# Pinning the up projection's products in program order on TensorE, and shifting on-chip memory from kept activations to raw weight buffers

## The chip, the cores and the metric

One core of a Trainium2 chip runs the whole kernel. The metric is the device time of one execution in microseconds (us). Three executions of the kernel before took 2089.94, 2092.08 and 2092.11 us; their median, 2092.08, is the time before. The engines are TensorE (PE, with its weight loads PEld), VectorE (DVE), ScalarE (ACT), GpSimd (POOL) and SyncE (SP); POOL and SP only issue DMAs where this change is concerned.

## The reference

One layer of an encoder: 512 tokens of 2048 features, in float32. The change touches only the gated MLP in the second half.

```python
xn = rms_norm(x, ffn_norm_g)                   # x: 512 x 2048
up = xn @ w_up                                 # w_up: 2048 x 11264
up = depthwise_conv(up, ffn_dw_w, ffn_dw_b)    # width 3, along the tokens
gate, val = split(up, 2)                       # 5632 channels each
x = x + (silu(gate) * val) @ w_down            # w_down: 5632 x 2048
return rms_norm(x, final_norm_g)
```

Ahead of it stand an input projection, a depthwise convolution and a neighbourhood attention, and an output projection.

## The kernel before

**Precision.** The products must come out in float32. A weight tile (`raw`, 128 x 1024, 512 KB) arrives by DMA. ACT rounds it into `whi` (L115), and DVE takes the remainder into `wlo` (L116), each 128 x 1024. Activations are split likewise. A product is then made of two or three matmuls: high by high, high by low, low by high. There are `NW` = 4 buffers for `whi` and for `wlo`, and `NR` = 7 for `raw`.

**The up projection.** A loop over 44 passes `f` (`hidden`, called in the loop near L747) makes 128 gate channels and 128 value channels for all 512 tokens in each. It doesn't multiply the blocks of weights and activations directly but uses seven products of sums of blocks, as in Strassen's scheme, in the order `TURN` = (3, 2, 4, 5, 1, 0, 6). The activation sums `xc` are made once and kept in SBUF. The weight sums are made by accumulating DMAs on POOL (L601) and additions on DVE (L611, L613). Each product but 2 takes eight steps `k` of two matmuls: L652 (`whi`, 512 columns) and L653 (`wlo`, 256 columns). Product 2 runs through the helper `mm3` (L126, L127, L128): eight steps of three matmuls of 256 columns.

**PSUM in a pass.** `ea` is one tile of two banks, whose halves are `pe` and `pa` (L637 to L639); `pd_`, `pb` and `pc_` are tiles of one bank. Products 3, 4 and 1 add up in `pa`, product 2 in `pc_`, 5 in `pd_`, 0 in `pe`, 6 in `pb`. After 3, 4 and 1, ACT copies what `pa` holds so far to `pd_`, `pe` and `pb` (`copied`, L660). After product 5 the two halves of `pd_` are added to the gate `g`; after product 0 `ea`, both its banks, to the value `vl`; and after product 6 `pb` to the rest of `g`. These folds are an ACT copy (L663) and a DVE addition (L664). ACT copies product 2's result to `w` (L670). So product 3 of the next pass writes `pa` only when the fold of `ea` has read it.

**What sets the order.** The kernel is written in program order, and a scheduler gives each engine its own order by priorities: it may move an instruction ahead of others if its operands are there. `shifted(-100)` raises the priority of the copies at L660. `pin` (`keep_in_program_order`) holds an instruction in its place among the pinned ones of its engine. Weights are asked for by `weights()`: whenever a product begins, the `whi` and `wlo` of the product `AHEAD` = 3 places later are made, and accumulating DMAs are begun `FAR` = 8 places ahead. `tick` and `done` put other work behind a product's last matmul: the steps that make the MLP's normalising factor in the first pass (statistics at L212, factors L215 to L225, L228), and the sums of the down projection's weights on POOL (L177, L180).

**The first pass.** The output projection ends just ahead of it, and the last of the `xc` that product 3 and the others multiply are still being made then (L542 on ACT, L543 on DVE).

**The MLP's activations.** A pass ends with the norm's factor, the convolution of width 3 and silu times value, which give one 2 KB tile per partition of `h` (128 x 512). The first 36 are stored to DRAM by SP (L708). The last `KEEP` = 8 stay in SBUF. In the last pass, POOL reloads the 36 (L741), up to eight behind each product. They come from a pool of `NT` = 79 tiles of 2 KB.

**The down projection** goes over 22 pairs of `h` in each of seven products (`TURN2`), kept pairs first (`order2`), with matmuls at L768 to L770. Its operand `ho` is made by `operand` (L730, L731) from `h` or from sums of halves of `h` (`hc`).

Of the kernel before, what the change touches and what calls it, by code (L numbers as in the profile page):

```python
# [39 lines left out]
KC0 = [0, 8, 24, 32]  # L40
H = S // 2
NK = NF // 2
KEEP = 8
NT = 79
NR = 7
AHEAD = 3
FAR = 8
NW = 4
# [22 lines left out]
def layer(ctx: ExitStack, tc: tile.TileContext, xT, w_in, w_out, w_up, w_down, par, tab, g3, out):  # L71
    nc = tc.nc
    consts = ctx.enter_context(tc.tile_pool(name="consts", bufs=1))
    wpool = ctx.enter_context(tc.tile_pool(name="w", bufs=3))
    tp = ctx.enter_context(tc.tile_pool(name="t", bufs=NT))
    sm = ctx.enter_context(tc.tile_pool(name="sm", bufs=2))
# [4 lines left out]
    @contextmanager  # L81
    def shifted(by):

        at = tc.cur_priority
        tc.cur_priority = max(at + by, 0)
        yield
        tc.cur_priority = at + (tc.cur_priority - max(at + by, 0))

    def t2(name, dt=F32):
        return tp.tile([P, S], dt, tag="t2k", name=name)  # L90

    def t4(shape, name):

        return wpool.tile(shape, F32, tag="raw", name=name, bufs=NR)

# [12 lines left out]
    def raw_unit(src, n):  # L108
        raw = t4([P, U * P], "raw")
        return raw, nc.sync.dma_start(raw[:, :n], src)  # L110

    def parts(raw, n):
        hi = wpool.tile([P, U * P], F32R, tag="whi", name="whi", bufs=NW)
        lo = wpool.tile([P, U * P], F32R, tag="wlo", name="wlo", bufs=NW)
        i = nc.scalar.activation(hi[:, :n], raw[:, :n], AF.Copy)  # L115
        j = nc.vector.tensor_sub(lo[:, :n], raw[:, :n], hi[:, :n].bitcast(F32))  # L116
        return hi, lo, i, j

    def unit(src, n):

        return parts(raw_unit(src, n)[0], n)[:2]

    def mm3(ps, w, wk, mh, ml, start, stop, more=False):
        hi, lo = w[:2]
        a = slice(wk * P, (wk + 1) * P)
        nc.tensor.matmul(ps, hi[:, a], mh, start=start, stop=False, skip_group_check=more)  # L126
        nc.tensor.matmul(ps, hi[:, a], ml, start=False, stop=False, skip_group_check=more)  # L127
        return nc.tensor.matmul(ps, lo[:, a], mh, start=False, stop=stop, skip_group_check=more)  # L128

# [3 lines left out]
    def tick(behind):  # L133
        for todo in (steps, asteps):
            while todo:
                try:
                    with tc.issue_after(behind.ins):
                        next(todo[0])
                    break
                except StopIteration:  # L140
                    todo.pop(0)
# [5 lines left out]
    def weights():  # L147
        at = weights.at
        weights.at += 1
        for i in range(at, min(at + 1 + FAR, len(plan))):  # L150
            if i in sums:
                sums.pop(i)()
        while len(made) < min(at + 1 + AHEAD, len(plan)):
            made.append(plan[len(made)]())
        return made[at]
# [90 lines left out]
    pin = tc.keep_in_program_order  # L246
    first = [w_in[n, :, u * U * P:(u + 1) * U * P] for u in range(KD // U) for n in (NC_, 0)]
    for k in range(KD):
# [6 lines left out]
        if k in (0, 2, 6, 15):  # L255
            raw, i = raw_unit(first[len(early)], U * P)
            pin(i)
            w = parts(raw, U * P)
# [6 lines left out]
    for step in ORDER:  # L265
        i = next(a_ if step == "a" else q_)
# [326 lines left out]
    def factors(f, at):  # L593

        def load(q):
            a["q", q] = raw_unit(w_up[f, q], U * P)[0]
            return a["q", q]

        def summed(c, q1, q2):
            a[c] = raw_unit(w_up[f, q1], U * P)[0]  # L600
            nc.gpsimd.dma_start(a[c], w_up[f, q2], accum_op=ALU.add)  # L601

        def make(c):
            if c in plain and ("q", plain[c]) not in a:
                load(plain[c])
            if c in plain:
                return a["q", plain[c]]
            if c == 1:
                return a[1]
            if c == 4:  # L610
                add(a[2], a[2], load(A22))  # L611
            elif c == 6:
                add(a[2], a[2], a["q", A12])  # L613
            return a[2]

        a = {}
        plain = {0: A22, 3: A11, 5: A12}
        sums[at + TURN.index(2)] = lambda: summed(2, A21, A11)
        sums[at + TURN.index(1)] = lambda: summed(1, A22, A21)
        return [lambda c=c: parts(make(c), U * P)[:2] for c in TURN]  # L620

    add = nc.vector.tensor_add
    for f in range(NF):
        plan.extend(factors(f, len(plan)))
    order2 = [*range(NK - KEEP // 2, NK), *range(NK - KEEP // 2)]
    def unit2(c, k):
        return unit(wsum[c][k] if c in wsum else w_down[k, {0: A22, 3: A11, 5: A12}[c]], U * P)
# [15 lines left out]
    def up(f, done):  # L643

        def product(c, ps, more):
            hi, lo = wt = weights()
            for k in range(U):
                m, w = comb[c][k], slice(k * P, (k + 1) * P)
                if c == 2:
                    i = mm3(ps[:, :H], wt, k, m[:, :H], m[:, H:], k == 0, k == U - 1)  # L650
                    continue
                nc.tensor.matmul(ps, hi[:, w], m, start=k == 0 and not more, stop=False, skip_group_check=more)  # L652
                i = nc.tensor.matmul(ps[:, :H], lo[:, w], m[:, :H], start=False, stop=k == U - 1,  # L653
                                     skip_group_check=more)
            tick(i)
            done(TURN.index(c), i)

        def copied(to, ps):
            with shifted(-100):
                nc.scalar.activation(to, ps, AF.Copy)  # L660

        def folded(to, ps):
            nc.scalar.activation(to, ps[..., H:], AF.Copy)  # L663
            add(to, to, ps[..., :H])  # L664

        product(3, pa, False)
        copied(pd_, pa)
        product(2, pc_, False)
        w = t2("w")[:, :H]
        nc.scalar.activation(w, pc_[:, :H], AF.Copy)  # L670
        product(4, pa, True)
        copied(pe, pa)
        product(5, pd_, True)
        g = t2("g")
        folded(g[:, :H], pd_)
        product(1, pa, True)
        copied(pb, pa)
        product(0, pe, True)
        v = t2("vl")
        by = v.rearrange("p (i t) -> p i t", i=2)  # L680
        folded(by, ea)
        add(by, by, w.unsqueeze(1).broadcast_to([P, 2, H]))
        product(6, pb, True)
        folded(g[:, H:], pb)
        return g, v
# [11 lines left out]
    hs = [None] * NF  # L697
    hd = [dram.tile([P, S], F32, name=f"h{f}") for f in range(NF - KEEP)]

    def hidden(f, done):  # L700
        g, v = up(f, done)
        nc.vector.tensor_mul(g, g, rstd2[0])
        nc.vector.tensor_mul(v, v, rstd2[0])
        g, v = conv3(g, f), conv3(v, NF + f)
        nc.scalar.activation(g, g, AF.Silu)
        nc.vector.tensor_mul(g, g, v)
        if f < NF - KEEP:
            nc.sync.dma_start(hd[f], g)  # L708
        else:
            hs[f] = g  # L710

    def operand(c, k):

        (b11, b12), (b21, b22) = ((hs[i][:, :H], hs[i][:, H:]) for i in (2 * k, 2 * k + 1))
        if c in (3, 5, 6):
            src = {3: b11, 5: b21, 6: b22}[c]
        else:
            t = t2("hc")
            src, m = t[:, :H], t[:, H:]
            if c == 2:  # L720
                nc.vector.tensor_sub(src, b22, b12)
            elif c == 1:
                nc.vector.tensor_sub(src, b11, b12)
            else:
                nc.vector.tensor_sub(m, b11, b12)
                nc.vector.scalar_tensor_tensor(src, b22, -1.0, m, op0=ALU.mult, op1=ALU.subtract)
                if c == 0:
                    nc.vector.scalar_tensor_tensor(src, src, -1.0, b21, op0=ALU.mult, op1=ALU.subtract)
        t = t2("ho", F32R)
        nc.scalar.activation(t[:, :H], src, AF.Copy)  # L730
        nc.vector.tensor_sub(t[:, H:], src, t[:, :H].bitcast(F32))  # L731
        return t

    back = [f for p in range(2) for f in range(p, NF - KEEP, 2)]

# [11 lines left out]
    for f in range(NF):  # L747
        hidden(f, again if f == NF - 1 else paced)
    assert not jobs and not open_job and not back

    def four(first):

        if first:
            b = psa.tile([P, 2, S], F32, tag="sc", name="pd2")
            return [b[:, 0], b[:, 1]] + [psa.tile([P, S], F32, tag="tr", name="pd", bufs=2) for _ in range(2)]
        return [psm.tile([P, S], F32, tag="mm", name="pd") for _ in range(3)] + [psa.tile([P, S], F32, tag="po",
                                                                                         name="pd")]
# [97 lines left out]
    a = four(True)  # L857
# [19 lines left out]
    a = four(True)  # L877
# [68 lines left out]
```

## Time and profile before

| | |
|---|---|
| median of three runs | 2092.08 us |
| the profiled execution, its span | 2091.84 us, 2090.1 us |
| mean granted clock of TensorE, as a share of full speed | 0.996 |
| DMA, mean over the span | 213 GB/s, 444.72 MB |
| up projection, about | 708 to 1656 us of the span |
| down projection, about | 1657 to 2082 us of the span |

How to read the rows: a row of the page's groups has the line, the engine, the operation, output and inputs with shapes and count, then busy time and mean ns of one, then the idle time of the engine just ahead of these instructions and what ended it (`<-`). A row of waits has the engine and line that waited, what ended the wait, the total in us, how many times and the longest. A row of the timeline has the start and the duration in us, the engine and line, and in brackets the idle time ahead and its releaser. Matmuls are pipelined: their rows overlap, and one that starts 0.12 us after another may be given 0.28 us.

### The profile page before, as it was taken

To read this page: it belongs to the slowest core of one execution; us is meant where nothing else is said; L and a number is where in the kernel's file an instruction comes from. 1 tells how busy PE (TensorE), PEld (TensorE's weight loads), DVE (VectorE), ACT (ScalarE), POOL (GpSimd) and SP (SyncE) were. 2 spreads that over 40 slices of the span, in tenths; PEclk is the share of its full clock that TensorE was granted. 3 is DMA by queue.
4 is the path that set the end of the run, shared out by engine and by line. 5 is a ranking of instruction groups with operands and counts; after the bars stand their busy time and mean duration, and the time that the engine had idled before them with its cause. 6 is when DMAs were issued, how large, how long until landed. Compare 5 with 4: busy or idle time off the path is not lost.

```text
span 2090.1 us, 28359 instructions
## 1 busy us (share of the span) xinstructions
PE 2015.7 (96%) x10511; PEld 1687.4 (81%) x10511; DVE 1602.6 (77%) x2267; ACT 1090.8 (52%) x1680; POOL 228.5 (11%) x314
## 2 busy tenths in 40 slices
PE   8999999999999999999999999999999999999997
PEld 6888888877788788888888888888888788888886
DVE  7985796686558787777878777787878798895765
ACT  6234424447426665555555555565655554554553
POOL 0111111110011111111111111111110300000000
PEclk9999999999999999999999999999999999999999
DMA  6777677767658788888888888888886776665563
GB/s 228 171 222 181 179 172 193 182 181 239 187 165 216 195 217 249 216 237 236 225 253 208 253 216 245 228 237 241 214 239 160 283 275 219 211 213 194 193 207 132
DMA packets 140859, 444.72 MB, mean 213 GB/s; under 512 B 15792, under 2 KB 23984, under 8 KB 139312
## 3 DMA queue, kind: packets, MB, share of 16 engines
q1 hardware_dynamic: 97776, 292.94, 40.4%
q0 software_dynamic: 42944, 149.97, 34.0%
q8 instruction: 82, 1.34, 0.2%
q14 instruction: 57, 0.47, 0.1%
HBM read 425.02 MB, written 110.10 MB: 256 GB/s over the span
## 4 chain that ended last, share of the span: by engine, by line
PE 74%; issue 20%; ACT 3%; DMA 1%; DVE 1%; POOL 0%; SPq 0%; POOLq 0%; DVEq 0%; ACTq 0%
PE pu L652 24%; PE pu L653 12%; PE pj L126 6%; PE pj L128 6%; PE pj L127 6%; PE po L126 3%; PE po L127 3%; PE po L128 3%; ACT whi L115 3%; PE pu L126 3%; PE pu L128 2%; PE pu L127 2%; PE po L450 1%; PE sc L410 1%; PE trp L437 1%
## 5 line engine op out<-in xcount | busy, mean ns | idle before, releaser
L115 ACT ACTIVATE whi<-raw 128x1024 fp32r<-128x1024 f32 x574 | 606.9, 1058 | 867.7 <-PE pu L652 310.7
L116 DVE TENSOR_TENSOR wlo<-raw,whi 128x1024 fp32r<-128x1024 f32 x574 | 697.2, 1221 | 377.3 <-ACT whi L115 354.5
L652 PE MATMUL pu<-xc,whi 128*128 128x512 f32 x2112 | 760.5, 403 | 1.5 <-ACT pu L660 1.5
L653 PE MATMUL pu<-xc,wlo 128*128 128x256 f32 x2112 | 593.1, 281 | 0.0
L652 PEld LDWEIGHTS pu<-xc,whi 128*128 128x128 f32 x2112 | 396.7, 188 | 103.8 <-ACT pu L660 9.9
L653 PEld LDWEIGHTS pu<-xc,wlo 128*128 128x128 f32 x2112 | 399.0, 189 | 0.3 <-issue 0.2
L126 PE MATMUL pj<-xh,whi 128*128 128x512 f32 x640 | 253.9, 398 | 8.7 <-ACT whi L115 8.7
L128 PE MATMUL pj<-xh,wlo 128*128 128x512 f32 x640 | 251.0, 392 | 0.6 <-DVE wlo L116 0.5
L127 PE MATMUL pj<-xl,whi 128*128 128x512 f32 x640 | 251.2, 393 | 0.0
L768 PE MATMUL pd<-whi,ho 128*128 128x512 f32 x616 | 240.2, 390 | 1.6 <-ACT ho L730 1.6
L770 PE MATMUL pd<-whi,ho 128*128 128x512 f32 x616 | 240.2, 390 | 0.6 <-DVE ho L731 0.6
L769 PE MATMUL pd<-wlo,ho 128*128 128x512 f32 x616 | 240.3, 390 | 0.0
L324 DVE SCALAR_TENSOR_TENSOR y<-ch,prm,y 128x507 f32<-128x507 f32 (+14 forms) x240 | 169.9, 741 | 3.3
L126 PEld LDWEIGHTS pj<-xh,whi 128*128 128x128 f32 x640 | 120.8, 189 | 37.1 <-ACT whi L115 10.1
L126 PE MATMUL pu<-xc,whi 128*128 128x256 f32 x352 | 104.2, 296 | 44.8 <-ACT whi L115 44.3
L601 POOL DMA_DIRECT2D raw<-in_w_up x88 | 89.5, 1017 | 507.6 <-DMA raw<-in_w_up 233.2
L128 PEld LDWEIGHTS pj<-xh,wlo 128*128 128x128 f32 x640 | 120.8, 189 | 27.9 <-DVE wlo L116 2.0
L127 PEld LDWEIGHTS pj<-xl,whi 128*128 128x128 f32 x640 | 120.9, 189 | 24.6 <-issue 0.7
L768 PEld LDWEIGHTS pd<-whi,ho 128*128 128x128 f32 x616 | 116.1, 188 | 26.4 <-ACT ho L730 1.9
L770 PEld LDWEIGHTS pd<-whi,ho 128*128 128x128 f32 x616 | 116.0, 188 | 25.1 <-DVE ho L731 1.1
L769 PEld LDWEIGHTS pd<-wlo,ho 128*128 128x128 f32 x616 | 116.0, 188 | 24.3 <-DVE wlo L116 0.3
L180 POOL DMA_DIRECT2D ws<-in_w_down x88 | 79.4, 903 | 503.4 <-DMA ws<-ws 257.4
(170 smaller groups left out, 2478.0 us busy)
## 6 DMA issues: line engine op xcount, KB each, us to landing
raw<-in_w_up SPq DMA_DIRECT2D x220, 512.0 KB, 6.0
ws<-in_w_down POOLq DMA_DIRECT2D x132, 512.0 KB, 6.2
raw<-in_w_up POOLq DMA_DIRECT2D x88, 512.0 KB, 8.1
raw<-ws SPq DMA_DIRECT2D x88, 512.0 KB, 3.6
raw<-in_w_in SPq DMA_DIRECT2D x80, 512.0 KB, 5.1
raw<-in_w_down SPq DMA_DIRECT2D x66, 512.0 KB, 3.6
ws<-ws POOLq DMA_DIRECT2D x44, 512.0 KB, 6.7
raw<-in_w_out SPq DMA_DIRECT2D x32, 512.0 KB, 4.9
```

The costliest lines, as they stand in the source:

```text
L115: i = nc.scalar.activation(hi[:, :n], raw[:, :n], AF.Copy)
L116: j = nc.vector.tensor_sub(lo[:, :n], raw[:, :n], hi[:, :n].bitcast(F32))
L126: nc.tensor.matmul(ps, hi[:, a], mh, start=start, stop=False, skip_group_check=more)
L127: nc.tensor.matmul(ps, hi[:, a], ml, start=False, stop=False, skip_group_check=more)
L128: return nc.tensor.matmul(ps, lo[:, a], mh, start=False, stop=stop, skip_group_check=more)
L324: nc.vector.scalar_tensor_tensor(y[:, a:b], h[:, a + j - PAD:b + j - PAD], prm[:, o + j:o + j + 1], y[:, a:b], op0=ALU.mult, op1=ALU.add)
L601: nc.gpsimd.dma_start(a[c], w_up[f, q2], accum_op=ALU.add)
L652: nc.tensor.matmul(ps, hi[:, w], m, start=k == 0 and not more, stop=False, skip_group_check=more)
L653: i = nc.tensor.matmul(ps[:, :H], lo[:, w], m[:, :H], start=False, stop=k == U - 1, skip_group_check=more)
L768: nc.tensor.matmul(ps[i], h[:, t], wh[:, d], start=start and not more, stop=False, skip_group_check=more)
L769: nc.tensor.matmul(ps[i], h[:, t], wl[:, d], start=False, stop=False, skip_group_check=more)
L770: return nc.tensor.matmul(ps[i], h[:, tl], wh[:, d], start=False, stop=stop, skip_group_check=more)
```

## The change

Three sizes are set anew: four `h` tiles are kept in place of eight (so 40 are stored and reloaded), the pool of 2 KB tiles has 75 in place of 79, and there are nine raw buffers of 4 KB in place of seven. The memory in SBUF is the same, 8 KB moved.

A list `tight` is filled in the first pass after product 3 and emptied after the last pass. While it holds something, the first matmul of every product is pinned, and in product 2 the first matmul of each of its eight steps. Product 3 of the first pass isn't pinned. `operand` no longer takes halves of both tiles of a pair where a product needs one.

```diff
-KEEP = 8
-NT = 79
-NR = 7
+KEEP = 4
+NT = 75
+NR = 9
...
+    tight = []
+
     def mm3(ps, w, wk, mh, ml, start, stop, more=False):
         hi, lo = w[:2]
         a = slice(wk * P, (wk + 1) * P)
-        nc.tensor.matmul(ps, hi[:, a], mh, start=start, stop=False, skip_group_check=more)
+        i = nc.tensor.matmul(ps, hi[:, a], mh, start=start, stop=False, skip_group_check=more)
+        if tight:
+            pin(i)
...
-                nc.tensor.matmul(ps, hi[:, w], m, start=k == 0 and not more, stop=False, skip_group_check=more)
+                i = nc.tensor.matmul(ps, hi[:, w], m, start=k == 0 and not more, stop=False, skip_group_check=more)
+                if k == 0 and tight:
+                    pin(i)
...
         product(3, pa, False)
+        tight[:] = [1]
         copied(pd_, pa)
...
-        (b11, b12), (b21, b22) = ((hs[i][:, :H], hs[i][:, H:]) for i in (2 * k, 2 * k + 1))
         if c in (3, 5, 6):
-            src = {3: b11, 5: b21, 6: b22}[c]
+            src = hs[2 * k + (c != 3)][:, H if c == 6 else 0:][:, :H]
         else:
+            (b11, b12), (b21, b22) = ((hs[i][:, :H], hs[i][:, H:]) for i in (2 * k, 2 * k + 1))
...
     for f in range(NF):
         hidden(f, again if f == NF - 1 else paced)
     assert not jobs and not open_job and not back
+    tight.clear()
```

Lines of the changed kernel that stand for those of before: L126, L127, L128 become L128, L131, L132; L652 and L653 become L656 and L659; L660 becomes L666, L663 and L664 become L669 and L670, L670 becomes L677, L601 becomes L605, L212, L225 and L228 become L216, L229 and L232. L110, L115 and L116 stay.

## The prediction

> **What bounds the kernel now.** I read the page's busy shares first, then the waits of TensorE, then the windows of the up projection, and last the timeline of one of its passes. The page:
>
> ```profile
> span 2090.1 us, 28359 instructions
> ...
> PE 2015.7 (96%) x10511; PEld 1687.4 (81%) x10511; DVE 1602.6 (77%) x2267; ACT 1090.8 (52%) x1680; POOL 228.5 (11%) x314
> ...
> L115 ACT ACTIVATE whi<-raw 128x1024 fp32r<-128x1024 f32 x574 | 606.9, 1058 | 867.7 <-PE pu L652 310.7
> ...
> L126 PE MATMUL pu<-xc,whi 128*128 128x256 f32 x352 | 104.2, 296 | 44.8 <-ACT whi L115 44.3
> ```
>
> TensorE is busy in 96% of the span, so a gain can only come from its 74 us of idle time (2090.1 - 2015.7), and anything that moves its matmuls away from those gaps costs. 44.8 us of the 74 stand ahead of one group, product 2 of the up projection. The waits of TensorE split that up:
>
> ```profile
> PE pu L126 <- ACT whi L115: 44.3, 43, 1.0
> ...
> PE pd L768 <- ACT ho L730: 1.6, 1, 1.6
> PE pu L652 <- ACT pu L660: 1.5, 1, 1.5
> ```
>
> 43 waits of 1.0 us, one for each pass but one of 44, and one single wait of 1.5 us at L652, on another releaser. There is no row in which TensorE waits for a raw weight tile of the up projection. The windows of the stage say that it is steady:
>
> ```profile
> 1000.00:1200.00 200.00, 189.70 (x1113) 163.97 (x1112) 156.62 (x186) 112.44 (x158) 30.47 (x38) 1.00 0.86 238
> 1200.00:1400.00 200.00, 190.74 (x1121) 165.24 (x1121) 156.94 (x186) 112.10 (x157) 30.25 (x38) 1.00 0.84 232
> ```
>
> The columns are window, length, busy time (and count) of PE, PEld, DVE, ACT and POOL, granted clock, DMA share, GB/s. Some 9.3 us in 200 are idle at full clock; DVE (157) and ACT (112) have room.
>
> The timeline of one pass, PE and then ACT, shows what stands around the 1.0 us:
>
> ```profile
> 1111.56 0.28 PE L653 MATMUL pu<-xc,wlo 128*128 128x256 f32 x1
> 1112.87 0.39 PE L126 MATMUL pu<-xc,whi 128*128 128x256 f32 x1 [1.03 <-ACT whi L115]
> 1113.09 0.28 PE L127 MATMUL pu<-xc,whi 128*128 128x256 f32 x1
> 1113.35 0.50 PE L652 MATMUL pu<-xc,whi 128*128 128x512 f32 x1
> ```
>
> ```profile
> 1111.76 1.06 ACT L115 ACTIVATE whi<-raw 128x1024 fp32r<-128x1024 f32 x1 [1.49 <-PE pu L652]
> 1112.72 0.58 ACT L660 ACTIVATE pu<-pu 128x512 f32<-128x512 f32 x1
> ```
>
> Product 1 ends with the L653 at 1111.56. ACT then makes a whi (its buffer came free with product 1's last L652), and behind it, in ACT's order, L660 copies product 1's result out of PSUM until 1113.30. Product 0 starts with the L652 at 1113.35. So product 0 waits for L660. The L126 and L127 at 1112.87 and 1113.09 belong to product 2 of the next pass, need only the fresh whi, and were slipped into the second half of the gap: **the row names the filler's wait; the gap itself is L660's.** The same happens once more per pass, ahead of the next pass's product 3:
>
> ```profile
> 1118.99 0.28 PE L653 MATMUL pu<-xc,wlo 128*128 128x256 f32 x1
> 1119.11 0.28 PE L128 MATMUL pu<-xc,wlo 128*128 128x256 f32 x1
> 1119.23 0.28 PE L126 MATMUL pu<-xc,whi 128*128 128x256 f32 x1
> 1119.35 0.48 PE L652 MATMUL pu<-xc,whi 128*128 128x512 f32 x1
> ```
>
> ```profile
> 1118.60 0.68 DVE L664 TENSOR_TENSOR vl<-vl,pu 128x512 f32<-128x512 f32 x1
> ```
>
> Product 6 ends at 1118.99 + 0.12, product 3 waits for the fold L664, over at 1119.28, and two more fillers cover the 0.24 us between.
>
> **The change part by part.**
>
> *The pins.* In the orders that the compiler gives the engines, before has four of product 2's 24 matmuls ahead of their place in 43 of the passes: one pair between products 1 and 0, one between products 6 and 3. After has all 24 behind product 3. The semaphores that the others wait for are the same in both programs: product 0's first matmul still waits for the copy L660 (L666 after), which still stands behind the same whi on ACT; product 3's first still waits for the fold L664 (L670). So both gaps stay as long as they are, and four matmuls that were free now cost their pitch. The pitch is that of the 20 that stand together:
>
> ```profile
> 1122.22 0.28 PE L127 MATMUL pu<-xc,whi 128*128 128x256 f32 x1
> ...
> 1124.48 0.28 PE L128 MATMUL pu<-xc,wlo 128*128 128x256 f32 x1
> ```
>
> (1124.48 - 1122.22) / 19 = 0.119 us. Four are 0.476 us, and 43 passes **+20.5 us**. The gap without fillers is already in this trace. The last pass has no next product 2 to borrow from:
>
> ```profile
> 1647.96 0.28 PE L653 MATMUL pu<-xc,wlo 128*128 128x256 f32 x1
> 1649.75 0.50 PE L652 MATMUL pu<-xc,whi 128*128 128x512 f32 x1 [1.52 <-ACT pu L660]
> 1650.09 0.28 PE L653 MATMUL pu<-xc,wlo 128*128 128x256 f32 x1
> ...
> 1650.44 0.28 PE L653 MATMUL pu<-xc,wlo 128*128 128x256 f32 x1
> ```
>
> From product 1's last matmul to product 0's first it takes 1649.75 - 1647.96 = 1.79 us there, without fillers, and 1113.35 - 1111.56 = 1.79 with them. They cost nothing where they stand, and taking them away gains nothing. After should show this 1.5 us row 44 times.
>
> *The first pass* is where the pins meet another gap. Product 3's last step waits for xc, the layer input's last combination; before fills with 22 matmuls of product 2:
>
> ```profile
> 711.08 0.36 PE L653 MATMUL pu<-xc,wlo 128*128 128x256 f32 x1
> 711.28 0.28 PE L126 MATMUL pu<-xc,whi 128*128 128x256 f32 x1
> ...
> 714.53 0.38 PE L126 MATMUL pu<-xc,whi 128*128 128x256 f32 x1 [0.59 <-ACT xc L542]
> 714.76 0.50 PE L652 MATMUL pu<-xc,whi 128*128 128x512 f32 x1
> ...
> 716.35 0.40 PE L652 MATMUL pu<-xc,whi 128*128 128x512 f32 x1
> ...
> 720.25 1.02 PE L228 MATMUL st<-dg,ones 128*128 128x512 f32 x2
> ```
>
> ```profile
> 719.06 0.87 DVE L225 TENSOR_SCALAR dg<-ident,rsy 128x128 f32<-128x128 f32 x4
> ```
>
> After, product 2 stands wholly behind that step, so TensorE stands from 711.4 to 714.76 (xc comes no earlier), does the statistics as before, and product 2's 24 from about 716.03, for 2.85 us, to 718.9. In its order the L228 comes next, ahead of product 4, and needs dg, which ends at 719.93. Product 4 thus begins behind L228, where before had 11 pairs of L652 and L653 done between 716.35 and 720.25. The loss is those 3.9 us less the 0.3 by which L228 starts earlier: **+3.6 us**.
>
> *Whether these idle times cost clock.* The row nearest to it is the start of the down projection:
>
> ```profile
> 1657.28 0.50 PE L768 MATMUL pd<-whi,ho 128*128 128x512 f32 x1 [1.61 <-ACT ho L730]
> ...
> 1658.62 0.80 PE L770 MATMUL pd<-whi,ho 128*128 128x512 f32 x1 [0.62 <-DVE ho L731]
> 1659.21 0.63 PE L768 MATMUL pd<-whi,ho 128*128 128x512 f32 x1
> ...
> 1662.51 0.39 PE L769 MATMUL pd<-wlo,ho 128*128 128x512 f32 x1
> ```
>
> ```profile
> 1660.00:1670.00 10.00, 10.00 (x42) 8.14 (x41) 8.43 (x14) 6.58 (x13) 4.52 (x10) 0.91 1.03 392
> ```
>
> After 1.61 + 0.62 us of idling with two matmuls between, matmuls took 0.63 in place of 0.39, at a pitch of 0.43 in place of 0.23, from 1658.62 to about 1661.8: 3.2 x (1 - 0.23/0.43) = 1.5 us lost. After the 1.52 us at 1649.75 the pairs went on at 0.35 at once (1650.09 to 1650.44), so one such gap alone costs no clock, and I take nothing per pass; both ends (0 and 1.5 us each) are kept as a rival. For the first pass's 3.3 us, 0 to 1.5, and I take 0, since what follows has its own 1 us wait for dg that would hide most of it. The Trainium skill, TensorE: Matmul & The Clock Gate, Part 1 (What's actually happening), has the clock halved after at least one idle window of about 3.4 us that runs freely; by it neither a 1.5 us gap nor, mostly, the first pass's would cost anything, and the sum stays. The trace speaks for a tighter gate than that: 2.2 us of idle in 3 were enough at 1658.62.
>
> *Nine raw buffers.* The row for whi on page says what ACT waits for: PE, 310.7 us, that is a free whi buffer, of which there are four before and after. Raw tiles come in ahead of it already. In the down projection ACT waited for them little:
>
> ```profile
> ACT whi L115 <- DMA raw<-in_w_down: 3.3, 2, 1.7
> ```
>
> and TensorE not at all. I take 0; at most 3.3 us could come back. The Trainium skill, Perfetto Trace Analysis (Optimization Strategy), says that the same bubble repeating on the engine to be saturated can mean too few buffers. By that rule 43 equal gaps would speak for the nine; the releasers agree that a buffer is short, but it is whi's.
>
> *Four tiles of h kept in place of eight.* Four more stores on SP and four more reloads on POOL, 256 KB each: 1 MB to read in a stretch that moves 392 GB/s (the window of 1660 above, DMA share 1.03), some 2.7 us of DMA, and two kept pairs in place of four to work on meanwhile: 12 matmuls of a unit x 0.23 = 2.7 us each, 5.5 us in place of 11. The reloads are issued product by product in the last pass, 20 us before the first is used, and two more raw tiles (5.4 us of work) lie ready; I take 0, bounds -3 and +6 (all 2.7 shown, and as much for the late raw tiles behind them). The subtraction of operands not needed by products 3, 5 and 6 is a matter of Python names and emits the same instructions.
>
> **Sum.** The profiled execution took 2091.84 us (span 2090.1 and 1.74 around it), 0.24 below the runs' median of 2092.08. 2091.84 + 20.5 + 3.6 = 2115.9: **2116 us, 1.15% slower.** Its own range: the four matmuls at 0.36 to 0.5 us a pass (if half of the 0.24 us at product 3 closes, or the fold comes a little later), 15 to 22; the first pass 2 to 5; the down projection -3 to +6: 2106 to 2125.
>
> **The rivals.**
>
> *The gap closes* (faster). If product 0 could start straight behind product 1, as the row "L126 <- ACT whi" taken by itself suggests, each pass would lose the 1.79 - 0.12 = 1.67 us between them, and pay the 0.24 at product 3 and four matmuls: before spends 1.67 + 0.24 there, after 0.24 + 0.476, a gain of 1.19 x 43 = 51, so 2091.8 - 51 + 3.6 = 2044. Half-way, if only L660 passed its whi on ACT (1.06 earlier), the gain is 1.06 - 0.48 = 0.58 a pass, 25 us: 2070. It decides in what L660 stands behind and whether product 0 waits for it. Against it: both are in the order of after, and the last pass's 1.52 us. Chance 0.06.
>
> *No change.* The pins don't bite, or what they cost per pass is given back by the chain of whi, which would have to move ahead by 0.48 us: 2092 to 2096. Against it: the order shows the four matmuls moved, and whi's buffers are released by the same matmuls. Chance 0.06.
>
> *The clock falls in each pass.* If gaps of 1.5 and 0.24 us every 21 us trip the gate as those at 1658 did: 43 x 1.5 = 64 more, 2180. Against it the row at 1650.09. Chance 0.04.
>
> *The tiles run short in the down projection.* Raw and h reloads share DMA engines that are full there (share 1.03), and TensorE comes to wait for an h once the kept pairs' 5.5 us are used up: if the four more reloads' 2.7 us, and as much of raw tiles held up behind them, stand on the path in one product or in two, it costs 5 to 10 us: 2121 to 2126. Chance 0.09.
>
> **How the numbers follow.** The forecast has 0.75, in 2106 to 2125. The range of 8 in 10 takes most of the tile case and a little beyond the low end: 2103 to 2127. Faster by over 0.2% (4.2 us, about what a measurement of this kernel can tell from no change): the first rival, 0.06. Within 0.2%: the second, 0.06. Slower: the forecast, the clock and the tiles, 0.88.
>
> **What would show it.** Right: in after's waits, "PE pu L126" (L128 there) gone, and "PE pu L652 <- ACT pu L660" (L656, L666) with 44 of some 1.5 us, 66 in all; a smaller second row of product 3 waiting for the vl fold, 43 of up to 0.24; a pass of 0.48 us more; PE busy in 200 us down by about 4. In the first pass, an idle stretch of 3.3 us at 711 and one of 1 us before the L228. Wrong: L666 ahead of the whi on ACT, product 0 straight behind product 1, a granted clock under 1.00 in the windows of the up projection, or waits for h or raw at L768's place.

## The result and the profile after

Four runs of the changed kernel took 2114.21 to 2120.74 us, median 2114.91, against 2092.1 (2089.94 to 2092.38) for before: a ratio of 1.0117, 95% interval 1.0098 to 1.0137. It is **1.2% slower**, 22.8 us; the forecast was 2116. The profiled execution took 2115.08 us, its span 2113.1.

The page after, and TensorE's waits:

```profile
span 2113.1 us, 28490 instructions
...
PE 2011.4 (95%) x10511; PEld 1682.2 (80%) x10511; DVE 1603.5 (76%) x2267; ACT 1091.4 (52%) x1680; POOL 230.1 (11%) x318
...
L656 PE MATMUL pu<-xc,whi 128*128 128x512 f32 x2112 | 758.8, 402 | 73.6 <-ACT pu L666 66.7
...
L128 PE MATMUL pu<-xc,whi 128*128 128x256 f32 x352 | 100.3, 285 | 0.0
```

```profile
PE pu L656 <- ACT pu L666: 66.7, 44, 1.5
...
PE pu L656 <- DVE xc L547: 3.3, 1, 3.3
...
PE pd L776 <- ACT ho L737: 1.6, 1, 1.6
```

```profile
PEld pu L656 <- DVE vl L670: 17.4, 43, 0.4
```

The idle time that stood ahead of product 2 (44.8 us) has gone from that row, and 73.6 us stand ahead of the first matmuls of the other products. The copy (L666) now ends 44 waits of 1.5 us, where the waits before name it once. The smaller wait of product 3 for the fold of the value stands in the rows of the weight loads, 43 times up to 0.4 us. The matmuls are as many as before and their busy time differs by 0.2%: no work was added, only cover taken away.

A window of 200 us, and the gap in one pass, PE and then ACT:

```profile
1200.00:1400.00 200.00, 185.65 (x1105) 160.78 (x1105) 155.00 (x184) 112.02 (x157) 29.88 (x37) 1.00 0.85 226
```

```profile
1123.39 0.28 PE L659 MATMUL pu<-xc,wlo 128*128 128x256 f32 x1
1125.18 0.49 PE L656 MATMUL pu<-xc,whi 128*128 128x512 f32 x1 [1.51 <-ACT pu L666]
```

```profile
1123.59 1.06 ACT L115 ACTIVATE whi<-raw 128x1024 fp32r<-128x1024 f32 x1 [1.49 <-PE pu L656]
1124.55 0.58 ACT L666 ACTIVATE pu<-pu 128x512 f32<-128x512 f32 x1
```

From product 1's last matmul to product 0's first it is 1.79 us, to the hundredth what it was with two fillers in between. ACT does the same two things in the same order at the same distance. TensorE is busy for 185.65 us of these 200, where it was 190.74, and the clock stayed at 1.00.

Where the 23.0 us of the two spans went, read at product 0's first matmul in the first and the last pass. Before:

```profile
727.29 0.50 PE L652 MATMUL pu<-xc,whi 128*128 128x512 f32 x1
```

and 1649.75 in the row of the last pass that the prediction shows. After:

```profile
731.16 0.50 PE L656 MATMUL pu<-xc,whi 128*128 128x512 f32 x1 [1.51 <-ACT pu L666]
```

```profile
1672.67 0.49 PE L656 MATMUL pu<-xc,whi 128*128 128x512 f32 x1 [1.51 <-ACT pu L666]
```

43 passes took 922.46 us before and 941.51 after: **+19.05**, or 0.443 a pass (21.45 to 21.90). Up to there the first pass and what lies ahead of it lost 3.87, and everything behind (2090.1 - 1649.75 = 440.35 and 2113.1 - 1672.67 = 440.43) lost 0.08. The 3.87 are two things: the stages ahead of the up projection ended 1.1 us earlier in this execution (its first matmul at 707.22 against 708.32), and the first pass itself lost **5.0**. TensorE in the first pass after, and then DVE's making of dg:

```profile
713.58 0.79 PE L656 MATMUL pu<-xc,whi 128*128 128x512 f32 x1 [3.25 <-DVE xc L547]
714.17 0.41 PE L659 MATMUL pu<-xc,wlo 128*128 128x256 f32 x1
714.38 1.70 PE L216 MATMUL st<-ones,acc 128*128 128x1 f32 x8
715.94 0.56 PE L128 MATMUL pu<-xc,whi 128*128 128x256 f32 x1
...
719.07 0.32 PE L132 MATMUL pu<-xc,wlo 128*128 128x256 f32 x1
719.23 0.28 PE L128 MATMUL pu<-xc,whi 128*128 128x256 f32 x1
...
720.30 1.02 PE L232 MATMUL st<-dg,ones 128*128 128x512 f32 x2
```

```profile
718.89 0.87 DVE L229 TENSOR_SCALAR dg<-ident,rsy 128x128 f32<-128x128 f32 x4
```

After 3.25 us of idling the matmuls are slow from the first one on, until 719.07: those of 0.28 us take 0.41, at a granted clock of 0.66 in the window of 710 to 720 us (its row is shown with the pins from the second pass on). dg is ready at 719.76, before product 2 ends. This 5.0 is one execution: two other kernels with the same order in the first pass lost 4.0 there, as the section on why the prediction was right shows.

### The profile page after: what moved, and what is told of

It is laid out like the page before. It is cut to its first block, busy times and chain, and to the rows that moved or that the text cites. A ratio compares the mean times of both kernels' runs of the same rounds, so it can differ in the third digit from the quotient of the medians.

```text
span 2113.1 us, 28490 instructions
## 1 busy us (share of the span) xinstructions
PE 2011.4 (95%) x10511; PEld 1682.2 (80%) x10511; DVE 1603.5 (76%) x2267; ACT 1091.4 (52%) x1680; POOL 230.1 (11%) x318
## 4 chain that ended last, share of the span: by engine, by line
PE 66%; issue 24%; ACT 5%; DVE 3%; DMA 2%; POOL 0%; SPq 0%; DVEq 0%; POOLq 0%; ACTq 0%
PE pu L656 21%; PE pu L659 9%; PE pj L128 6%; PE pj L132 6%; PE pj L131 6%; ACT whi L115 3%; PE po L128 3%; PE po L132 3%; PE po L131 3%; PE pu L128 2%; PE pu L131 2%; PE pu L132 2%; DVE vl L670 1%; ACT pu L666 1%; PE po L454 1%
## 5 line engine op out<-in xcount | busy, mean ns | idle before, releaser
L115 ACT ACTIVATE whi<-raw 128x1024 fp32r<-128x1024 f32 x574 | 607.1, 1058 | 886.4 <-PE pu L656 331.2
L116 DVE TENSOR_TENSOR wlo<-raw,whi 128x1024 fp32r<-128x1024 f32 x574 | 697.3, 1221 | 398.8 <-ACT whi L115 375.8
L656 PE MATMUL pu<-xc,whi 128*128 128x512 f32 x2112 | 758.8, 402 | 73.6 <-ACT pu L666 66.7
L659 PE MATMUL pu<-xc,wlo 128*128 128x256 f32 x2112 | 591.8, 280 | 0.0
L656 PEld LDWEIGHTS pu<-xc,whi 128*128 128x128 f32 x2112 | 396.7, 188 | 192.6 <-ACT pu L666 80.7
L659 PEld LDWEIGHTS pu<-xc,wlo 128*128 128x128 f32 x2112 | 398.9, 189 | 0.3 <-issue 0.2
L128 PE MATMUL pj<-xh,whi 128*128 128x512 f32 x640 | 253.4, 397 | 8.3 <-ACT whi L115 8.3
L132 PE MATMUL pj<-xh,wlo 128*128 128x512 f32 x640 | 250.4, 392 | 0.6 <-DVE wlo L116 0.6
L131 PE MATMUL pj<-xl,whi 128*128 128x512 f32 x640 | 250.7, 392 | 0.0
L128 PEld LDWEIGHTS pj<-xh,whi 128*128 128x128 f32 x640 | 120.7, 189 | 36.5 <-ACT whi L115 9.6
L132 PEld LDWEIGHTS pj<-xh,wlo 128*128 128x128 f32 x640 | 120.5, 188 | 27.9 <-DVE wlo L116 2.1
L131 PEld LDWEIGHTS pj<-xl,whi 128*128 128x128 f32 x640 | 120.7, 189 | 24.6 <-issue 0.7
L605 POOL DMA_DIRECT2D raw<-in_w_up x88 | 82.5, 937 | 486.7 <-DMA raw<-in_w_up 284.0
L128 PE MATMUL pu<-xc,whi 128*128 128x256 f32 x352 | 100.3, 285 | 0.0
```

Source lines behind the costliest of these rows:

```text
L128: i = nc.tensor.matmul(ps, hi[:, a], mh, start=start, stop=False, skip_group_check=more)
L656: i = nc.tensor.matmul(ps, hi[:, w], m, start=k == 0 and not more, stop=False, skip_group_check=more)
```

## The experiments

Two theories were set against each other first: that the loss is all in the matmuls that lost their place in a gap (the fillers), in the passes and in the first of them, and that the tiles and buffers share in it.

### The pins alone, and the buffers alone

The pins alone are the changed kernel with the sizes of before:

```diff
-KEEP = 4
-NT = 75
-NR = 9
+KEEP = 8
+NT = 79
+NR = 7
```

> The pins alone, with the sizes of before (eight tiles of h kept, 79 small tiles, seven raw buffers). Theory of the fillers: all of the loss is in the four matmuls of product 2 that lose their place in a gap (19 us over 43 passes) and in the first pass (5 us, less 1 that the stages ahead gained), so the time is that of the changed kernel, 2114 to 2117 us, and the waits of TensorE show the copy ahead of product 0 with 44 of 1.5 us. Rival, the buffers: if the smaller number of kept tiles or the shifted loads cost part of it, this run is below 2111 by that part, and the next one above before by the same.

Measured: 2114.18 us (2110.79 to 2114.76), 1.0108 of before (1.0094 to 1.0122), with 66.8 us in the wait for the copy. The pins alone make the time of the whole change. In this execution a pass takes (1674.11 - 730.66) / 43 = 21.94 us, a little more than the 21.90 of the whole change:

```profile
730.66 0.50 PE L656 MATMUL pu<-xc,whi 128*128 128x512 f32 x1 [1.51 <-ACT pu L666]
...
1674.11 0.50 PE L656 MATMUL pu<-xc,whi 128*128 128x512 f32 x1 [1.52 <-ACT pu L666]
```

The buffers alone are the changed kernel without the line that fills `tight`:

```diff
-        tight[:] = [1]
```

> The sizes alone (four tiles of h kept, 75 small tiles, nine raw buffers), and no pins. Theory of the fillers: 2090 to 2093 us, the same as before within 0.2%; the profile shows the 43 waits of 1.0 us ahead of product 2's moved matmuls as before, and the down projection starts and ends as before. The 1.2 us that the first 714 us of the changed kernel took less should be seen here, if the raw buffers gave them, and should be missing if they are scatter. Rival, the buffers: above 2096.

Measured: 2091.78 us (2088.65 to 2095.23), 1.0005 of before (0.9996 to 1.0014). Its waits are those of before:

```profile
PE pu L128 <- ACT whi L115: 44.3, 43, 1.0
...
PE pu L656 <- ACT pu L666: 1.5, 1, 1.5
```

Nine raw buffers and four kept tiles are worth nothing that can be measured, either way. Its up projection began at 708.76, with the same nine buffers that the changed kernel had at 707.22, so the 1.1 us ahead of the up projection were scatter, and not the raw buffers' doing.

### The pins from the second pass on

```diff
-        tight[:] = [1]
+        tight[:] = [1] if f else []
```

> The change with the pins beginning in the second pass in place of the first. Theory: product 2 of the first pass may again fill the wait for the last xc, so that the first pass costs no 5.1 us (3.9 of matmuls that nothing covers, and the rest from the half clock after 3.3 us of idling, less what the wait for dg hid); 19 us of the passes stay: 2109 to 2111. Rival: what the first pass loses is made up later (by the first waits of the second pass, which are set by ACT and DVE): 2114 to 2116, as the changed kernel.

Measured: 2110.46 us (2110.39 to 2112.59), 1.0097 (1.0081 to 1.0112). That is 4.5 us under the changed kernel's 2114.91, which was measured beside other runs of before (2092.1 there, 2090.51 here), and 3.7 under the pins alone, measured beside the same ones: the first pass's loss is real and stays to the end. A pass takes 21.89 us, as in the changed kernel. The 3.3 us wait is gone from its waits, and the mean clock of 710 to 720 us is 1.00, where the changed kernel has 0.66 (first this kernel's row, then the changed one's):

```profile
710.00:720.00 10.00, 9.47 (x65) 8.44 (x64) 8.30 (x24) 8.70 (x17) 0.92 (x1) 1.00 0.70 151
```

```profile
710.00:720.00 10.00, 6.75 (x35) 6.46 (x34) 7.39 (x23) 5.91 (x14) 0.92 (x1) 0.66 0.69 148
```

### All pins but one

Beside the edit of the run before:

```diff
-        if tight:
+        if tight and wk:
             pin(i)
```

> Pins from the second pass on, on every product's first matmul and on product 2's steps 1 to 7, but not on product 2's step 0. The instruction order then has the four fillers back in both gaps of a pass. Theory: one pin, of product 2's first matmul, makes the whole loss of the passes, and the time is that of before: 2089 to 2094. Rival: the pins of the other products cost too: between 2094 and 2110.

Measured: 2092.28 us (2086.26 to 2096.63), 1.0012 (1.0001 to 1.0023), with a pass of 21.44 us (21.45 before) and again 43 waits of 1.0 us ahead of product 2. All that the passes lose hangs on one pin, of product 2's first matmul. The order of the matmuls also says what `pin` does more exactly than the text ahead of the prediction: it holds an instruction behind the one that precedes it in the program on its engine. Freed, step 0 goes ahead into the gaps, and step 1, pinned behind step 0, follows it there.

### What holds the gap open

The prediction held that the gap is a conversion (`whi`) and, behind it on ACT, a copy that product 0 waits for. Four kernels change one link each.

**The order on ACT.** All conversions and copies are pinned on ACT, so that the copy comes first:

```diff
         i = nc.scalar.activation(hi[:, :n], raw[:, :n], AF.Copy)
+        if tight:
+            pin(i)
...
-                nc.scalar.activation(to, ps, AF.Copy)
+                i = nc.scalar.activation(to, ps, AF.Copy)
+            if tight:
+                pin(i)
```

> Pins from the second pass on, as in the run of 2110 us, and on ACT the copies and the conversions of weights pinned too, so that the copy after product 1 stands ahead of the conversion that it stood behind. One tile of two banks as before. Theory: the gap is that conversion and then the copy; without the 1.06 us of conversion ahead of it, it shrinks from 1.5 to 0.7 us, 44 times (35 us), and the fold of the value, also no longer behind a conversion, is ready before product 6 ends, which closes the 0.22 us ahead of product 3 and its slow first matmul (up to 14 us): 2058 to 2078. Rival: product 0 waits for the conversion itself, or for something behind it: 2108 to 2112.

Measured: 2208.96 us, 1.0578 (1.0562 to 1.0594): a miss by 130 us, and no answer to the question. The gap in question did shrink as foreseen, to 0.73 us, but the pins changed more than the one pair. They held the copy after product 3 behind a conversion too, and ACT came to it late: in the pass shown it first copies product 2's result (1123.43), for which it waits until product 2 has ended. So a gap of 2.56 us opened ahead of product 4 in all passes but the first two, and a pass took 23.97 us on average in place of 21.89:

```profile
PE pu L658 <- ACT pu L668: 140.7, 86, 2.7
```

```profile
1111.77 0.50 PE L658 MATMUL pu<-xc,whi 128*128 128x512 f32 x1 [0.73 <-ACT pu L668]
...
1125.95 0.80 PE L658 MATMUL pu<-xc,whi 128*128 128x512 f32 x1 [2.56 <-ACT pu L668]
1126.55 0.41 PE L661 MATMUL pu<-xc,wlo 128*128 128x256 f32 x1
1126.76 0.63 PE L658 MATMUL pu<-xc,whi 128*128 128x512 f32 x1
```

```profile
1123.43 0.38 ACT L681 ACTIVATE w<-pu 128x256 f32<-128x256 f32 x1 [1.13 <-PE pu L134]
...
1124.37 1.04 ACT L115 ACTIVATE whi<-raw 128x1024 fp32r<-128x1024 f32 x1
1125.32 0.58 ACT L668 ACTIVATE pu<-pu 128x512 f32<-128x512 f32 x1
```

**One conversion only.** The mended form, with the pins on TensorE from the second pass on, pins on ACT only the conversion made when product 0 begins, that is behind the copy:

```diff
+        if late:
+            pin(i)
         j = nc.vector.tensor_sub(lo[:, :n], raw[:, :n], hi[:, :n].bitcast(F32))
...
+        late[:] = [1]
         product(0, pe, True)
+        late.clear()
```

> The mended form of the run that pinned all of ACT: pins on TensorE from the second pass on (2110 us by itself), and on ACT only one conversion of a pass pinned, the one made for product 0's call for weights, behind the copy after product 1 instead of ahead of it. The orders show that the copy after product 3 is left where it was, and that the fold of the value now stands ahead of its conversion too. Theory: the gap is conversion and copy; 1.5 us become 0.7, 44 times (35 us less), and the wait ahead of product 3 closes (0.22 us and a slow first matmul, up to 14 us less): 2061 to 2077. Rival: the copy isn't what opens the gap: 2108 to 2112.

Measured: 2063.19 us (2061.78 to 2071.49), 0.9882 (0.9861 to 0.9904). 47 us come from the order on ACT alone, the rest of the program being that of 2110.46 us. The copy now goes straight behind product 1, and the wait that was 66.7 us is 32.1:

```profile
PE pu L660 <- ACT pu L670: 32.1, 44, 0.7
```

```profile
1107.55 0.58 ACT L670 ACTIVATE pu<-pu 128x512 f32<-128x512 f32 x1 [1.68 <-PE pu L663]
1108.04 1.05 ACT L117 ACTIVATE whi<-raw 128x1024 fp32r<-128x1024 f32 x1
...
1111.31 0.60 ACT L673 ACTIVATE vl<-pu 128x512 f32<-128x512 f32 x1 [2.21 <-PE pu L663]
```

That wait gives 34.6 of the 47 us. The fold of the value (L673) goes straight behind product 0 likewise, and the wait of product 3 for it, 43 times in the weight loads of the changed kernel, is not in this kernel's list of waits any more. By the timeline a pass takes 20.83 us in place of 21.89, and 0.31 us of that difference, 13 us in all, lies around that wait: between product 6's first matmul and product 4's.

**A fifth pair of split weights.** The conversion waits for product 1 because it needs the buffer that product 1 reads. Without pins, and with the change's 8 KB spent on a fifth pair instead of on raw buffers:

```diff
-NR = 9
+NR = 7
...
-NW = 4
+NW = 5
...
-        tight[:] = [1]
```

> No pins, and the 8 KB that come free with four kept tiles go to a fifth pair of split weights in place of two raw buffers (seven raw). Theory: the conversion that the copy stood behind waited for the last matmul of product 1 only because there were four of them; with five it is over before, the copy runs at once, and six fillers of 0.12 us cover what is left. Time per pass from 21.45 to 20.0 to 20.4 us: 2028 to 2050. Rival: the raw buffers are what is short, or the wait moves on: 2085 or more, as the run with nine raw buffers.

Measured: 2036.29 us (2034.65 to 2037.55), 0.9744 (0.9731 to 0.9757). A pass takes 20.21 us, within the 20.0 to 20.4 foreseen, and the copy begins straight behind product 1, with no conversion between them:

```profile
1107.53 0.58 ACT L666 ACTIVATE pu<-pu 128x512 f32<-128x512 f32 x1 [1.68 <-PE pu L659]
1108.34 1.06 ACT L115 ACTIVATE whi<-raw 128x1024 fp32r<-128x1024 f32 x1 [0.23 <-DVE raw L615]
```

The same 8 KB give 2.6% as split weights and nothing as raw ones.

**Two tiles instead of one.** Product 0 adds up in `pe` and the copy reads `pa`: two banks of one tile. With a tile for each, on the kernel before:

```diff
-    pe, pa = ea[:, 0], ea[:, 1]
+    pe, pa = psa.tile([P, S], F32, tag="po", name="pu"), ea[:, 1]
...
-        folded(by, ea)
+        folded(by[:, 0], pe)
+        folded(by[:, 1], pa)
```

> Before, with the two banks that product 0 and product 1 add up in held as two tiles of one bank each instead of one tile of two; the fold of the value is done for each bank by itself (two ACT copies and two DVE additions of 256 columns in place of one each of 512). Nothing is pinned. Theory: product 0 waits for the copy only because both banks are one tile; with two tiles it starts straight behind product 1. A pass then loses no 1.67 us between products 1 and 0 and perhaps not the 0.24 ahead of product 3, and runs its four fillers in product 2 (0.48 us): 1.2 to 1.43 us less a pass, 52 to 63 in all, 2029 to 2040 us, and the waits of TensorE in the up projection go to under 10 us. Rival 1: the gap is bounded by ACT (whi, then copy), and the wait moves to product 6, which needs the copy: then at most some 10 us are gained, 2080 or more. Rival 2: TensorE's writes to one bank while ACT reads its neighbour cost time: the pitch of product 0's matmuls grows.

Measured: 2018.96 us (2017.74 to 2019.24), 0.9655 (0.9642 to 0.9668), the fastest of all, 3.4% under before. TensorE is busy throughout the up projection, and of its waits there only the first pass's is left:

```profile
PE pu L126 <- ACT xc L542: 0.6, 1, 0.6
```

```profile
1200.00:1400.00 200.00, 200.00 (x1211) 177.25 (x1210) 170.70 (x212) 125.39 (x182) 33.61 (x42) 1.00 0.93 252
```

A pass takes 19.84 us (from the timeline, product 2's start at 732.66 in the second pass and 1565.93 in the last, 42 passes apart). That is 1.6 us less than before, where 1.2 to 1.43 were expected: the first pair of matmuls after a gap takes 0.46 us in place of 0.35 (the rows of 1113.35 and 1113.81), twice a pass, which the expectation had left out. The edit splits the fold as well as the tile, so the part of the gain that lies ahead of product 3 (about 0.3 us a pass) can be due to either; between products 1 and 0 no fold stands. Nothing is lost by ACT reading one bank while TensorE fills its neighbour: the pairs of product 0 go on at 0.35 us through the copy.

```profile
1122.03 0.40 PE L652 MATMUL pu<-xc,whi 128*128 128x512 f32 x1
...
1122.38 0.40 PE L652 MATMUL pu<-xc,whi 128*128 128x512 f32 x1
...
1122.74 0.40 PE L652 MATMUL pu<-xc,whi 128*128 128x512 f32 x1
```

```profile
1122.02 0.58 ACT L660 ACTIVATE pu<-pu 128x512 f32<-128x512 f32 x1
```

The Trainium skill, PSUM — Partial Sum Buffer (Summary: rules for kernel authors), has PSUM guarded by bank: a reader and a running matmul want different banks. Here they have them in both kernels, and these rows show that it costs the matmuls nothing; what made product 0 wait was the program's own semaphore, for a tile of two banks.

### The split tile with the change on top

With the changed kernel whole, pins and sizes:

> The changed kernel, pins and buffers and all, with product 0's and product 1's banks as two tiles. If a pin costs only where a gap stands open ahead of the pinned matmul, then without the gaps the pins of the passes cost nothing, and only the first pass's 5 us stay: 2019 (the split tile without pins) + 5 = 2024, 2022 to 2027. Rival: pins cost by themselves (an order that the weights' arrival doesn't suit): 2038 (19 us more) or so.

Measured: 2024.15 us (2023.24 to 2024.55), 0.9686 (0.9672 to 0.9699): the split tile's time and 5.2 us more. A pass takes 19.84 us here as in the split tile without pins, so the pins of the passes cost nothing; the first pass takes 4.0 us longer by the timeline, and the rest is scatter. With only the sizes, no pins:

> The split tile without pins, and with the changed sizes (four kept, 75 small tiles, nine raw buffers). TensorE is busy all the time in the up projection there, and DMA's share is 0.92 where it was 0.85. Theory: raw tiles are not short even so, and the time is that of the split tile alone, 2017 to 2021. Rival: with a pass of 19.8 us the loads become tight, and nine raw buffers give something, or the reloads cost something: outside of 2014 to 2024.

Measured: 2020.24 us (2018.62 to 2027.4), 0.968 (0.9659 to 0.9701): no gain from more raw buffers even at a DMA share of 0.93. So a pin is free where no gap stands ahead of the pinned matmul; it costs what it keeps out of a gap.

## Why the prediction was right, and where it was off

- **The gap is the copy's, not the conversion's row's.** Right. Which releaser a row names depends on which matmul stands first behind the gap. The waits after name the copy, 44 times 1.5 us, as forecast; that the conversion ahead of the copy makes a part of the gap is shown by the run with one conversion moved (1.5 to 0.73 us), and that the copy makes the rest by the split tile, which has no gap.
- **Four matmuls a pass.** Forecast 20.5 us, measured 19.05 in the profiled execution of the change (0.443 us a pass and not 0.476), 19.0 with the pins from the second pass on, and 21.0 with the pins alone (21.94 a pass). So the mechanism was right, and the size is right within what executions differ by. Where the four matmuls stand, from product 3's first matmul to product 4's, a pass grew by 0.486 us (from 5.301 to 5.787, means of 42 passes). The rest of the pass is 0.04 shorter: the gap ahead of product 3 is 0.34 us from start to start where it was 0.36 with its fillers (1118.99 to 1119.35); the other 0.02 I can't assign.

```profile
1108.90 0.28 PE L659 MATMUL pu<-xc,wlo 128*128 128x256 f32 x1
1109.24 0.50 PE L656 MATMUL pu<-xc,whi 128*128 128x512 f32 x1
```

- **The first pass.** Forecast 3.6 us, with nothing for the clock. From the up projection's first matmul to product 0's it took 18.97 us before and 23.94 after, 5.0 more; in the pins alone 23.00, 4.0 more; in the split tile with pins 21.25 against 17.26 without, 4.0 again. This is the step that was mis-sized, by 0.4 to 1.4. I had weighed the clock at 0 to 1.5 us and taken 0, because a wait of 1 us for dg would hide most of it. The clock fell in all three executions, but not at the same point. In the pins alone the statistics still ran at full speed, and product 2 was slow:

```profile
714.54 0.95 PE L216 MATMUL st<-ones,acc 128*128 128x1 f32 x8
...
719.80 1.02 PE L232 MATMUL st<-dg,ones 128*128 128x512 f32 x2
```

```profile
718.38 0.87 DVE L229 TENSOR_SCALAR dg<-ident,rsy 128x128 f32<-128x128 f32 x4
```

dg was ready at 719.25, no later after the stage's start than before, and product 2 ended 0.55 us behind it, at 719.80. Its 24 matmuls took 4.45 us there (715.35 to 719.80) in place of 2.85, and the wait for dg hid the larger part of these 1.6, as I had argued. In the profiled execution of the change the clock was low from the first matmul behind the gap. The statistics, from which dg is made, took 1.56 us where they took 0.81 before (714.38 to 715.94, 715.22 to 716.03). So dg itself came 0.9 us later after the stage's start (719.76 - 707.22 = 12.54, before 719.93 - 708.32 = 11.61), and product 2 ended 0.5 us behind even that, at 720.30. These 0.9 and 0.5 are the 1.4. A wait for dg can't hide what delays dg.

- **Nothing from nine raw buffers, nothing lost by four kept tiles.** Right: 0.08 us behind the up projection, and 1.0005 for the buffers alone. The pins alone, with the eight kept tiles of before, took 438.9 us for the same stretch, 1.5 less than before: there the clock didn't fall behind the idle 1.61 and 0.62 us at the start of the down projection (1.00 from 1680 to 1690 us, where the changed kernel has 0.83). The 1.5 us are what the prediction had read for that fall.
- **The clock doesn't fall in each pass.** Right for gaps of 1.5 us. That it can fall in a loop was shown by the run with all of ACT pinned, at 2.56 us.
- **The faster rival** was possible, but not by this change: it needed product 0 to start without the copy. The split tile did that, and gave 72 us (2018.96 against 2090.51) where the rival had 51 less the 3.6 of the first pass. Its half-way form, the copy ahead of the conversion on ACT, was put at 0.58 us a pass; the run with one conversion moved has 0.63 (21.45 before, 20.83), though it took a pin on ACT that the change doesn't have.

## What to carry to other kernels

A row of waits names what the instruction at the head of the queue waited for; where a scheduler has slipped work into a gap, that is the filler's wait. Look for the first instruction that can't be moved, or for a pass without fillers, before you pin anything: pins keep the gap and lose its cover. Then ask whether the wait is a true dependence; here splitting a tile of two banks was worth 3.4%, a fifth pair of split weights in place of two raw buffers 2.6%, and one conversion moved behind a copy on ACT 2.2% of the kernel without that pin. The pins on TensorE gained nothing in any of these runs.

## What the runs showed of the hardware

The clock was the surprise. Gaps of 1.5 us, 44 of them, never lowered it. One of 3.3 us (3.25 to 3.31) did so in all three executions that have it: at once and for 5.5 us in the changed kernel (713.58 to 719.07), 1.4 us behind the gap and for 3.4 us in the pins alone, 1.6 us behind it and for 3.3 us in the split tile with pins. And 42 gaps of 2.56 to 2.69 us in one kernel were followed by slow matmuls in 10 passes and not in the other 32. The gap ahead of 1102.29 was followed by pairs at 0.35 us, the next one by pairs at 0.64, at a granted clock of 0.77:

```profile
1102.75 0.39 PE L658 MATMUL pu<-xc,whi 128*128 128x512 f32 x1
...
1103.09 0.40 PE L658 MATMUL pu<-xc,whi 128*128 128x512 f32 x1
```

```profile
1126.76 0.63 PE L658 MATMUL pu<-xc,whi 128*128 128x512 f32 x1
...
1127.40 0.63 PE L658 MATMUL pu<-xc,whi 128*128 128x512 f32 x1
```

```profile
1120.00:1130.00 10.00, 7.44 (x41) 6.60 (x40) 7.80 (x10) 5.88 (x8) 0.00 (x0) 0.77 0.74 154
```

The Trainium skill, TensorE: Matmul & The Clock Gate, Part 1 (What's actually happening), has the window run freely; that the same gap halves the clock in some passes and not in others, and at once in one execution and later in another, agrees with that. The one idle window of some 3.4 us that it asks for does not fit: 3.3 us were enough in three executions of three, 2.56 us at times, and so were, in 7 of the 11 executions that have them, the 1.6 and 0.6 us with two matmuls between them at the start of the down projection; in the other 4 the matmuls behind them kept their speed. Where the limit for a single gap lies between 1.5 and 2.56 us, no run here tells.
